# A small copy ahead of ScalarE's loads, and every second rounding moved to GpSimd

## Chip, core and metric

The kernel runs on one core of a Trainium2 chip. The metric is the device time of one execution in microseconds (us); smaller is better. Before the change the median of three runs is 163.75 us (163.68 to 163.84).

## What is computed

A linear layer with a low-rank addition (LoRA with a diagonal), on 16 x 2048 = 32768 rows of 256 float32 numbers:

```python
def reference(x, W, lora_A, lora_B, lora_E, scale):
    x_flat = x.reshape(-1, in_dim)          # 32768 x 256
    y = x_flat @ W                          # W: 256 x 256
    lora_out = x_flat @ lora_A              # 256 x 16
    lora_out = lora_out * lora_E
    lora_out = lora_out @ lora_B            # 16 x 256
    y = y + scale * lora_out
    return y.reshape(batch, seq_len, out_dim)
```

Input and output are 33.5 MB each, so at least 67 MB pass between the chip's memory (HBM) and the core's on-chip memory (SBUF).

## The kernel before

The low-rank part is folded into the weights once: weff = W + A · diag(E · scale) · B (lines 177 to 191 and 238 to 246). Then out = x · weff, so each row of x goes through the core once.

Each of the 128 partitions handles 256 rows of x, which are cut into six blocks (BLOCKS, line 11). They pass through one ring in SBUF, which has room for 184 rows per partition (RING, line 12); a "row" below is one row per partition, 128 KB in all. A result overwrites its input's place in the ring, and the store is issued from there.

All large transfers stand in one list, ORDER (line 13), which SyncE issues from top to bottom: "L16" loads the next 16 rows, "S64" stores the next 64, "W" loads the weights. Three kinds of waits lie in it:

- a store waits until ScalarE has written the last of its rows (semaphore s_c, line 140);
- the load of row 184, the first that reuses places of the ring, waits until the first store has landed (line 137); the load of rows 240 to 255 waits for the second store;
- at the end SyncE waits for all stores of the last four pieces (line 263).

```python
ORDER = [
    "L8", "W", "L8", "L16", "L16", "L16", "L16", "L16", "L24", "L24", "L16", "L24",
    "S64", "S32",
    "L8", "L16", "L16", "L16", "L16",
    "S64", "S24", "S40", "S32",
]
```

Ahead of the list stands a group of early transfers (lines 115 to 120): the first load on SyncE's queue, and lora_A, lora_E and lora_B on ScalarE's queue.

Compute goes by steps of eight rows (G), 32 in all. In each step:

1. VectorE (DVE) rounds eight rows of the ring from float32 to bfloat16, into one of two buffers xb (line 167). It waits for the load where a step begins one.
2. TensorE (PE) transposes them, in eight transposes into PSUM (line 212); pairs of bfloat16 travel as one float32. The last of them counts up s_t.
3. VectorE copies the result from PSUM into one of two buffers xt (line 172).
4. TensorE multiplies by weff, sixteen products per step (line 228).
5. ScalarE copies the products from PSUM into the ring, four rows at a time (line 202), and counts up s_c where a store's rows end.

TensorE's order is fixed by a loop (lines 251 to 256): transposes of step n+1 always come before the products of step n. VectorE's order is: copy of step n, rounding of step n+2 (lines 193 to 195). The buffers are handed over by tokens that TensorE takes and returns (k_x, k_t, k_y). GpSimd (POOL) only makes the identity matrix for the transposes at the start (lines 145 to 155).

The change and the steps of the prediction touch the early group (115), the loop that issues ORDER (129), rounded (158), copied (169) and the loop that calls both (193).

Of the kernel before, what the change touches and what calls it, by code (L numbers as in the profile page):

```python
# [11 lines left out]
RING = 184  # L12
# [6 lines left out]
G = 8  # L19
H = 4  # L20
# [3 lines left out]
def kernel(  # L24
# [10 lines left out]
    nc = tc.nc  # L35
# [4 lines left out]
    x_flat = x.flatten_outer_dims()  # L40
    out_flat = out.flatten_outer_dims()
# [19 lines left out]
    xbs = [const.tile([P, G, K], BF16, name=f"xb_{i}") for i in range(2)]  # L61
# [22 lines left out]
    sem = lambda name: tc.alloc_semaphore(name)  # L84
    s_load = {f: sem(f"load_{f}") for f, _ in loads}

    s_last = sem("stores")
    s_store = {f: sem(f"store_{f}") for f, _ in stores if f < ROWS - RING}
# [4 lines left out]
    s_t, s_m, s_c = sem("s_t"), sem("s_m"), sem("s_c")  # L93
    k_x, k_t, k_y = ([sem(f"{k}_{i}") for i in range(2)] for k in ("k_x", "k_t", "k_y"))
    s_setup = sem("s_setup")

    def rows_of(flat, f, n):
        first, rows = block_of[f]
        block = flat[first * P:(first + rows) * P, :].rearrange("(p b) k -> p b k", b=rows)
        return block[:, f - first:f - first + n, :]  # L100

    def place(f, n):
        return ring[:, f % RING:f % RING + n, :]

    steps = list(range(0, ROWS, G))
    NS = len(steps)
# [2 lines left out]

    def load(f, n):
        return nc.sync.dma_start(out=place(f, n), in_=rows_of(x_flat, f, n)).then_inc(s_load[f], 16)

    early = [
        load(*loads[0]),
        nc.scalar.dma_start(out=a_sb, in_=lora_A.rearrange("(p c) r -> p c r", c=KC)).then_inc(s_in, 16),
        nc.scalar.dma_start(out=e_sb, in_=lora_E[:, None]).then_inc(s_in, 16),
# [7 lines left out]

    with tc.tile_critical():  # L127

        for kind, f, n in queue[1:]:
            if kind == "W":  # L130
                nc.sync.dma_start(
                    out=w_sb, in_=W.rearrange("(p c) m -> p c m", c=KC)
                ).then_inc(s_w, 16)
            elif kind == "L":
                for g, m in stores:
                    if g < f + n - RING and f - RING < g + m and g in s_store:
                        nc.sync.wait_ge(s_store.pop(g), 16)
                load(f, n)
            elif kind == "S":
                nc.sync.wait_ge(s_c, stores.index((f, n)) + 1)  # L140
                nc.sync.dma_start(out=rows_of(out_flat, f, n), in_=place(f, n)).then_inc(
                    s_store.get(f, s_last), 16
                )

        nc.gpsimd.memset(ident_f, 0.0).then_inc(s_setup, 1)  # L145
        nc.gpsimd.wait_ge(s_setup, 1)
        nc.gpsimd.affine_select(  # L147
            out=ident_f,
            in_=ident_f,
            compare_op=mybir.AluOpType.not_equal,  # L150
            fill=1.0,
            base=0,
            pattern=[[-1, P]],
            channel_multiplier=1,
        ).then_inc(s_setup, 1)


        def rounded(n):

            if n == NS:  # L160

                nc.vector.sem_inc(k_x[n % 2], 1)
            if n >= NS:
                return
            if steps[n] in s_load:
                nc.vector.wait_ge(s_load[steps[n]], 16)
            nc.vector.tensor_copy(out=xbs[n % 2], in_=place(steps[n], G)).then_inc(k_x[n % 2], 1)  # L167

        def copied(n):

            nc.vector.wait_ge(s_t, n + 1)
            nc.vector.tensor_copy(  # L172
                out=xts[n % 2].rearrange("p g r c -> p (g r c)"),
                in_=pts[n % 2].rearrange("p g r -> p (g r)").bitcast(BF16),
            ).then_inc(k_t[n % 2], 1)

        nc.vector.wait_ge(s_in, 48)
        nc.vector.tensor_copy(out=b_bf, in_=b_sb)  # L178
        nc.vector.wait_ge(s_setup, 3)
        nc.vector.tensor_scalar(  # L180
            out=ate,
            in0=ps_at,
            scalar1=e_sb,
            scalar2=float(scale),
            op0=mybir.AluOpType.mult,
            op1=mybir.AluOpType.mult,
        ).then_inc(s_setup, 1)
        rounded(0)
        nc.vector.wait_ge(s_w, 16)
        nc.vector.wait_ge(s_setup, 5)  # L190
        nc.vector.tensor_add(out=weff, in0=w_sb, in1=ps_aeb).then_inc(s_setup, 1)  # L191
        rounded(1)
        for n in range(NS):
            copied(n)
            rounded(n + 2)


        for k in k_y:
            nc.scalar.sem_inc(k, 1)
        for h in range(ROWS // H):  # L200
            nc.scalar.wait_ge(s_m, h + 1)
            nc.scalar.copy(out=place(h * H, H), in_=pys[h % 2]).then_inc(k_y[h % 2], 1)  # L202
            if (h + 1) * H in store_ends:
                nc.scalar.drain().then_inc(s_c, 1)  # L204


        def take(token):
            nc.tensor.wait_ge(token, 1).then_inc(token, -1)  # L208


        def transpose(b, j):
            return nc.tensor.transpose(  # L212
                pts[b][:, j, :], xbs[b][:, j, :].bitcast(FP32), ident_f
            )

        def transposes(b):
            take(k_x[b])
            for j in range(G):
                t = transpose(b, j)
            t.then_inc(s_t, 1)  # L220

        def products(b):
            take(k_t[b])
            for j in range(G):
                if j % H == 0:
                    take(k_y[j // H])
                for c in range(KC):
                    m = nc.tensor.matmul(  # L228
                        pys[j // H][:, j % H, :],
                        xts[b][:, j, :, c],  # L230
                        weff[:, c, :],
                        start=(c == 0),
                        stop=(c == KC - 1),
                    )
                if j % H == H - 1:
                    m.then_inc(s_m, 1)

        nc.tensor.wait_ge(s_setup, 2)
        nc.tensor.wait_ge(s_in, 48)
        for c in range(KC):  # L240
            t = nc.tensor.transpose(ps_at[:, c, :], a_sb[:, c, :], ident_f)  # L241
        t.then_inc(s_setup, 1)
        nc.tensor.wait_ge(s_setup, 4)
        for c in range(KC):
            m = nc.tensor.matmul(ps_aeb[:, c, :], ate[:, c, :], b_bf, start=True, stop=True)  # L245
        m.then_inc(s_setup, 1)
        transposes(0)
        nc.tensor.wait_ge(s_setup, 6)
        left = nc.tensor.alloc_register("left")
        nc.tensor.reg_mov(left, NS // 2)  # L250
        with nc.tensor.While(left):
            transposes(1)
            products(0)
            transposes(0)
            products(1)
            nc.tensor.reg_sub(left, left, 1)

        total = nc.sync.alloc_register("total")
        nc.sync.reg_mov(total, n_last)
# [39 lines left out]
```

## Time and profile before

| What | us |
|---|---|
| median of three runs | 163.75 |
| the profiled execution's own time | 163.49 |
| its span, first to last instruction | 161.7 |
| PE busy | 91.0 (56% of the span) |
| DVE busy | 76.4 (47%) |
| ACT busy | 63.1 (39%) |
| POOL busy | 0.7 |
| moved by DMA | 67.42 MB, 417 GB/s over the span |

How to read it: the page is one execution under the hardware profiler; its durations are set against its own 163.49 us, which is 0.26 us below the median of the runs. An engine's share of busy time tells little by itself. What matters is what ends last in each stretch, and whether an engine's wait delays anything behind it. Names such as SPq or ACTq are the sequencers that issue DMAs and waits; q1 is SyncE's DMA queue, q10 ScalarE's.

### The profile page before, as it was taken

The numbers are of one execution on the slowest core, as the hardware profiler recorded it, in microseconds if no ns is written. First come the engines' busy times: TensorE is split into PE (matmuls) and PEld (weight loads), VectorE is DVE, ScalarE is ACT, GpSimd is POOL, SyncE is SP. The second block draws the span as 40 slices with busy tenths as digits, with TensorE's granted clock in tenths as the row PEclk, the third lists the DMA queues.
The fourth block names the chain that finished last, engine by engine and source line by source line (L and its number), as shares of the span: only waits on it lengthen the run. The fifth ranks groups of instructions, "written<-read, shape, count | busy, mean of one in ns | idle before, by whom it ended". The sixth has DMA issues, their size and how long they took to land. (4 is left out here: it accounts for less than half of the span.)

```text
span 161.7 us, 1972 instructions
## 1 busy us (share of the span) xinstructions
PE 91.0 (56%) x780; PEld 81.5 (50%) x780; DVE 76.4 (47%) x67; ACT 63.1 (39%) x65; POOL 0.7 (0%) x6
## 2 busy tenths in 40 slices
PE   0188999999999999970000079999994000000000
PEld 0066899999799999960000066999993000000000
DVE  0296999985889988800000048999930000000000
ACT  3004486868586868680000005768685000000000
POOL 1000000000000000000000000000000000000000
PEclk9999999999999999996555558999999555555555
DMA  5999999999999999799699999999899799899992
GB/s 179 417 426 450 413 434 442 417 458 426 432 415 438 432 521 456 324 519 470 300 413 407 440 421 446 424 421 571 357 486 470 340 395 488 381 466 442 405 421 113
DMA packets 3522, 67.42 MB, mean 417 GB/s; under 512 B 560, under 2 KB 576, under 8 KB 704
## 3 DMA queue, kind: packets, MB, share of 16 engines
q1 hardware_dynamic: 3312, 67.37, 97.6%
q10 hardware_dynamic: 208, 0.03, 0.1%
q14 instruction: 2, 0.02, 0.0%
HBM read 33.85 MB, written 33.55 MB: 417 GB/s over the span
## 5 line engine op out<-in xcount | busy, mean ns | idle before, releaser
L202 ACT COPY ring<-py 128x1024 f32<-128x1024 f32 x64 | 61.8, 1017 | 58.6 <-PE py L228 58.5
L228 PE MATMUL py<-weff,xt 128*128 128x256 bf16 x512 | 62.2, 275 | 0.7 <-PEq L208 0.7
L228 PEld LDWEIGHTS py<-weff,xt 128*128 128x128 bf16 x512 | 50.5, 99 | 7.4 <-issue 1.5
L167 DVE CAST xb<-ring 128x2048 bf16<-128x2048 f32 x32 | 39.0, 1220 | 31.8 <-DMA ring<-in_x_dram 31.5
L212 PE MATMUL pt<-ident_f,xb 128*128 128x128 f32 x264 | 36.7, 286 | 24.0 <-PEq L208 23.9
L212 PEld LDWEIGHTS pt<-ident_f,xb 128*128 128x128 f32 x264 | 31.7, 148 | 25.9 <-issue 25.6
L172 DVE COPY xt<-pt 128x2048 bf16<-128x2048 bf16 x32 | 39.1, 1221 | 4.5 <-PE pt L212 4.4
L241 PE MATMUL py<-ident_f,a_sb 128*16 128x128 f32 x2 | 0.6, 396 | 6.8 <-DMA b_sb<-in_lora_B_dram 6.8
L241 PEld LDWEIGHTS py<-ident_f,a_sb 128*16 128x16 f32 x2 | 0.1, 88 | 6.8 <-issue 6.8
L178 DVE CAST b_bf<-b_sb 16x256 bf16<-16x256 f32 x1 | 0.3, 282 | 6.7 <-DMA b_sb<-in_lora_B_dram 6.7
L202 ACT ACT_TABLE_LOAD x1 | 1.3, 1283 | 2.4 <-issue 2.4
L245 PE MATMUL py<-b_bf,ate 16*128 16x256 bf16 x2 | 0.6, 402 | 0.6 <-DVE ate L180 0.6
L180 DVE TENSOR_SCALAR ate<-py,e_sb 16x256 bf16<-16x256 f32 x1 | 0.5, 472 | 0.5 <-PE py L241 0.5
L191 DVE TENSOR_TENSOR weff<-w_sb,py 128x512 bf16<-128x512 f32 x1 | 0.7, 669 | 0.0
L245 PEld LDWEIGHTS py<-b_bf,ate 16*128 16x128 bf16 x2 | 0.1, 104 | 1.1 <-DVE ate L180 1.1
L147 POOL TENSOR_SCALAR_AFFINE_SELECT ident_f<-ident_f 128x128 f32<-128x128 f32 x1 | 0.3, 294 | 0.2 <-POOL ident_f L145 0.2
L145 POOL MEMSET ident_f<- 128x128 f32 x1 | 0.2, 205 | 1.0 <-SPq L127 1.0
L280 POOL MEMSET const-bfloat16-1.0<- 128x1 bf16 x1 | 0.1, 102 | 0.0
L280 POOL MEMSET const-uint8-127<- 128x1 uint8 x1 | 0.1, 102 | 0.0
L280 POOL MEMSET const-float32-0.0<- 128x1 f32 x1 | 0.1, 99 | 0.2 <-issue 0.2
L280 POOL MEMSET const-float32-1.0<- 128x1 f32 x1 | 0.1, 99 | 0.0
## 6 DMA issues: line engine op xcount, KB each, us to landing
ring<-in_x_dram SPq DMA_DIRECT2D x10, 2048.0 KB, 21.3
ring<-in_x_dram SPq DMA_DIRECT2D x3, 3072.0 KB, 42.5
out_dram<-ring SPq DMA_DIRECT2D x2, 4096.0 KB, 40.0
out_dram<-ring SPq DMA_DIRECT2D x1, 5120.0 KB, 37.4
ring<-in_x_dram SPq DMA_DIRECT2D x3, 1024.0 KB, 7.2
out_dram<-ring SPq DMA_DIRECT2D x1, 3072.0 KB, 39.1
w_sb<-in_W_dram SPq DMA_DIRECT2D x1, 256.0 KB, 5.1
out_dram<-ring SPq DMA_DIRECT2D x2, 43.1
```

The costliest lines, as they stand in the source:

```text
L147: nc.gpsimd.affine_select(out=ident_f, in_=ident_f, compare_op=mybir.AluOpType.not_equal, fill=1.0, base=0, pattern=[[-1, P]], channel_mul ...
L167: nc.vector.tensor_copy(out=xbs[n % 2], in_=place(steps[n], G)).then_inc(k_x[n % 2], 1)
L172: nc.vector.tensor_copy(out=xts[n % 2].rearrange("p g r c -> p (g r c)"), in_=pts[n % 2].rearrange("p g r -> p (g r)").bitcast(BF16),).the ...
L178: nc.vector.tensor_copy(out=b_bf, in_=b_sb)
L180: nc.vector.tensor_scalar(out=ate, in0=ps_at, scalar1=e_sb, scalar2=float(scale), op0=mybir.AluOpType.mult, op1=mybir.AluOpType.mult,).the ...
L191: nc.vector.tensor_add(out=weff, in0=w_sb, in1=ps_aeb).then_inc(s_setup, 1)
L202: nc.scalar.copy(out=place(h * H, H), in_=pys[h % 2]).then_inc(k_y[h % 2], 1)
L212: return nc.tensor.transpose(pts[b][:, j, :], xbs[b][:, j, :].bitcast(FP32), ident_f)
L228: m = nc.tensor.matmul(pys[j // H][:, j % H, :], xts[b][:, j, :, c], weff[:, c, :], start=(c == 0), stop=(c == KC - 1),)
L241: t = nc.tensor.transpose(ps_at[:, c, :], a_sb[:, c, :], ident_f)
L245: m = nc.tensor.matmul(ps_aeb[:, c, :], ate[:, c, :], b_bf, start=True, stop=True)
L280: nc = _bacc.Bacc("TRN2", target_bir_lowering=False, num_devices=1)
```

## The change

It has two parts.

First, a transfer from x in HBM straight into out in HBM, 64 KB in 16 pieces of 4 KB, stands first in ScalarE's queue. It covers the first 64 rows of 256 numbers, all of which the first store writes again; so that store waits for the copy (semaphore s_in0).

Second, GpSimd does the rounding of steps 3, 5, 7 and so on to 31; VectorE keeps the even steps and step 1. GpSimd waits for the transposes of the step that last used the buffer (s_t) and for the load. The token that VectorE gave after the last step stays.

The list freed takes the place of a pop from s_store; SyncE's transfers and their other waits are in the same order as before.

```diff
     early = [
+        nc.scalar.dma_start(out=out_flat[0:16 * H, :].rearrange("(p b) k -> p b k", b=H),
+                            in_=x_flat[0:16 * H, :].rearrange("(p b) k -> p b k", b=H)).then_inc(s_in0, 16),
         load(*loads[0]),
...
+        freed = []
...
-                    if g < f + n - RING and f - RING < g + m and g in s_store:
-                        nc.sync.wait_ge(s_store.pop(g), 16)
+                    if g < f + n - RING and f - RING < g + m and g not in freed:
+                        freed.append(g)
+                        nc.sync.wait_ge(s_store[g], 16)
                 load(f, n)
             elif kind == "S":
+                if f == 0:
+                    nc.sync.wait_ge(s_in0, 16)
                 nc.sync.wait_ge(s_c, stores.index((f, n)) + 1)
...
+        seen = []
+
+        def caster(n):
+            return nc.gpsimd if n % 2 == 1 and n >= 3 else nc.vector
+
+        def rounded(n, engine):
+            piece = max(f for f in s_load if f <= steps[n])
+            waits = [(s_load[piece], 16)]
+            for sem_, count in waits:
+                if (engine, sem_) not in seen:
+                    seen.append((engine, sem_))
+                    engine.wait_ge(sem_, count)
+            engine.tensor_copy(out=xbs[n % 2], in_=place(steps[n], G)).then_inc(k_x[n % 2], 1)
+
+        for n in range(NS):
+            if caster(n) is nc.gpsimd:
+                nc.gpsimd.wait_ge(s_t, n - 1)
+                rounded(n, nc.gpsimd)
...
         for n in range(NS):
             copied(n)
-            rounded(n + 2)
+            if n + 2 < NS and caster(n + 2) is nc.vector:
+                rounded(n + 2, nc.vector)
+            elif n + 2 == NS:
+                nc.vector.sem_inc(k_x[NS % 2], 1)
```

More of the change, by code (lines that the diff above doesn't have):

```diff
@@ L95 @@
     s_setup = sem("s_setup")
+    s_in0 = sem("s_in0")
     def rows_of(flat, f, n):
@@ L155 @@
         ).then_inc(s_setup, 1)
[L158 to L167, printed above, removed]
+        seen = []
[13 more added lines that the diff above has]
+                rounded(n, nc.gpsimd)
         def copied(n):
@@ L187 @@
         ).then_inc(s_setup, 1)
-        rounded(0)
+        rounded(0, nc.vector)
         nc.vector.wait_ge(s_w, 16)
@@ L191 @@
         nc.vector.tensor_add(out=weff, in0=w_sb, in1=ps_aeb).then_inc(s_setup, 1)
-        rounded(1)
+        rounded(1, nc.vector)
         for n in range(NS):
             copied(n)
-            rounded(n + 2)
+            if n + 2 < NS and caster(n + 2) is nc.vector:
+                rounded(n + 2, nc.vector)
+            elif n + 2 == NS:
+                nc.vector.sem_inc(k_x[NS % 2], 1)
         for k in k_y:
```

## The prediction

> **What bounds the kernel now.** I read the slices of the page and its table of DMA queues first, because the kernel moves 67 MB and does little arithmetic on each byte:
>
> ```profile
> DMA  5999999999999999799699999999899799899992
> ...
> q1 hardware_dynamic: 3312, 67.37, 97.6%
> q10 hardware_dynamic: 208, 0.03, 0.1%
> ```
>
> The 16 DMA engines are busy from the first slice to the last, and SyncE's queue (q1) alone fills 97.6% of their span. ScalarE's queue (q10) carries almost nothing. Next the busy time by stretches of the span; the columns are PE, PEld, DVE, ACT, POOL, granted clock, DMA share, GB/s:
>
> ```profile
> 4.00:58.00 54.00, 48.70 (x417) 43.52 (x418) 44.55 (x41) 31.17 (x33) 0.00 (x0) 1.00 1.01 431
> 58.00:90.00 32.00, 13.62 (x125) 12.41 (x123) 9.46 (x9) 11.24 (x12) 0.00 (x0) 0.75 0.99 425
> 112.00:160.00 48.00, 10.99 (x101) 9.97 (x99) 6.07 (x6) 9.31 (x10) 0.00 (x0) 0.64 0.96 415
> ```
>
> The rate is 431 GB/s while PE works nearly all the time and 415 GB/s when PE is idle for three quarters of it: the transfers don't wait for compute. Third, the packet records under this view. Packets of one size take one time (8 KB 309 ns, 2 KB 84 ns, 64 KB 2418 ns) and each engine starts one where the one before ended. The first packet starts at 1.77 us; the engines end between 158.7 and 160.2 us. So **the time is one stream of packets on each engine**, and an edit counts only if it lengthens that stream, moves its start, or leaves it empty.
>
> The page's chain that ended last (PE L228 9%, PE L212 4%) stops at 124.1 us, with ScalarE's last copy; the remaining 36 us are the stores in flight. SyncE's waits say the same; columns are total us, times, longest:
>
> ```profile
> SPq L141 <- ACTq L204: 70.2, 5, 26.9
> SPq L113 <- DMA out_dram<-ring: 39.6, 2, 33.4
> SPq L263 <- DMA out_dram<-ring: 35.8, 1, 35.8
> ```
>
> The 70.2 us look alarming but are waits ahead of a full queue. How full, the timeline of ScalarE (end of a block's last copy, after which its store is issued) against the packet records tells:
>
> ```profile
> 33.41 1.93 ACT L202 COPY ring<-py 128x1024 f32<-128x1024 f32 x2 [0.69 <-PE py L228]
> ...
> 70.78 1.93 ACT L202 COPY ring<-py 128x1024 f32<-128x1024 f32 x2 [0.69 <-PE py L228]
> 97.65 2.08 ACT L202 COPY ring<-py 128x1024 f32<-128x1024 f32 x2 [24.95 <-PE py L228]
> ...
> 122.16 1.93 ACT L202 COPY ring<-py 128x1024 f32<-128x1024 f32 x2 [0.69 <-PE py L228]
> ```
>
> The first store (64 rows) is issued at 35.4 us and its first packet starts at 59.5: 24 us of cover. The second is issued at 46.6 and starts at 78.8: 32 us. The fifth (40 rows) is ready at about 113.6 and starts at 137.0: 23 us. The last is issued at 124.1 and starts at 149.1: **25 us**. Between 72.7 and 97.65 compute stands still because the ring is full (the load of row 184 lands at about 92), which is another 19 us of cover for the first ten of the moved casts.
>
> **The change part by part.**
>
> *GpSimd casts.* 15 of 32 casts (steps 3, 5, ... 31) move from DVE to POOL. DVE loses 15 x 1.220 = 18.3 us of work. That is worth nothing: PE sets the pace of compute, as the chain shows,
>
> ```profile
> 102.04 0.87 PE pt L212 x8
> 102.91 1.75 PE py L228 x16
> ```
>
> so a step is 0.87 + 1.75 = 2.62 us, two are 5.24, and even compute is hidden. What POOL needs for a cast of 128 x 2048 no row of before shows. The nearest rows:
>
> ```profile
> L167 DVE CAST xb<-ring 128x2048 bf16<-128x2048 f32 x32 | 39.0, 1220 | 31.8 <-DMA ring<-in_x_dram 31.5
> ...
> L147 POOL TENSOR_SCALAR_AFFINE_SELECT ident_f<-ident_f 128x128 f32<-128x128 f32 x1 | 0.3, 294 | 0.2 <-POOL ident_f L145 0.2
> L145 POOL MEMSET ident_f<- 128x128 f32 x1 | 0.2, 205 | 1.0 <-SPq L127 1.0
> L280 POOL MEMSET const-bfloat16-1.0<- 128x1 bf16 x1 | 0.1, 102 | 0.0
> ```
>
> One element costs POOL 0.10 us and 128 cost 0.205, so 0.8 ns each after the first: 0.1 + 2048 x 0.0008 = 1.8 us. By the affine select, (294 - 102) / 127 = 1.5 ns each: 3.2 us. With nothing fixed, 16 x 294 ns = 4.7 us. Ends 1.2 (DVE's row) and 4.7; I take 3.2, the one POOL row that reads and writes. The new wait: POOL's cast of step n waits for the transposes of step n-2 (s_t) and its load. Nothing but later casts is queued behind it on POOL. Those who wait for it are PE's transposes of n, and behind them PE's products of n-1. From the end of transposes n-2 to the start of transposes n PE does two sets of products and one of transposes: 1.75 + 0.87 + 1.75 = 4.37 us. 3.2 us fit. At 4.7, with some 0.3 for hand-overs, a pair of steps becomes 0.87 + 5.0 = 5.9 instead of 5.24: 15 x 0.65 = 10 us of compute later, inside the cover. Cost: **0**. Without cover each us by which a pair grows costs 15 us.
>
> The Trainium skill (SBUF — State Buffer, "Who interferes with whom") speaks against moving a cast: GpSimd and a DVE instruction in a 2-port mode exclude each other for a whole instruction. No run shown has both at work, so this trace can't tell. By it one DVE cast (1.22 us) per pair would stand ahead of POOL's, and as an estimate the pair would be 0.87 + 0.3 + 4.7 + 1.22 = 7.1 us, which the cover still absorbs, so the sum stays.
>
> *The copy.* ScalarE issues one DMA more, ahead of three that took 0.41, 0.45 and 0.44 us, so those and what follows move by about 0.45 us: b_sb lands at 7.1 instead of 6.7, DVE's first work and the table load (2.44 us) shift likewise. All of that is compute, under 24 us of cover: 0. SyncE's queue isn't passed by it. The new wait of SyncE (s_in0 ahead of the first store) is met some 30 us early.
>
> The transfer itself has no cover: it runs on the same engines. The DMA view of the first 5 us has 138 packets of q10 among 143 of q1, so the queues share the engines. 16 pieces of 4 KB are one packet on each engine. Between 84 ns (2 KB) and 309 ns (8 KB), 4 KB take 84 + 225/3 = **0.16 us**. But it writes HBM in the midst of loads, and a turn of direction has a price in the packets: where the loads first give way to stores (57.4 to 58.8 us), 14 of the 24 KB packets took 0.09 to 0.31 us more than 0.914, in all 2.5 us, or **0.16 us** per engine. The next such turn (110 us) cost one engine 0.33 and the others nothing. So the turn is 0 to 0.33; I take 0.16, because the copy is the first write to out, as the first turn was. The worst row is the start: first packets of 8 KB took 0.4 to 1.03 us instead of 0.309, some 0.47 over on the mean; if the copy pays this anew, it costs 0.16 + 0.47 = 0.63, at the worst 0.16 + 0.72 = 0.9. If it takes that delay over from the load, and early, it costs less than nothing: 0.16 - 0.47 = -0.3.
>
> *Bookkeeping.* The list freed replaces pop; SyncE's waits and transfers stay in order: 0.
>
> Sum: 163.49 (profiled execution; span 161.7 and 1.8 around it) + 0.16 + 0.16 = 163.81. The median of the runs is 0.26 above the profiled one, so **164.07, rounded 164.1 us**. A measurement of this kernel tells about 0.2% (0.33 us) from no change; the forecast lies on that edge, and I count it as slower.
>
> **The rivals.**
> 1. *The copy is only its bytes, or hides in part*: no turn is paid, 0 to +0.2 us, 163.75 to 163.95. For it: 128-byte packets of q10 among loads take 13 ns, so queues are mixed without a stall. Against it: these write SBUF, not HBM.
> 2. *The copy takes over the cold start (other side)*: 16 descriptors may reach the engines sooner than the load's 128; then the 0.47 us that first packets lose run before the load, and the stream starts smoothly: -0.3 to -0.5, 163.25 to 163.45. It decides if the copy's packets start at least 0.3 us ahead of 1.77. Against it: both queues issue at 0.74 us, and q10's first packet in before came 0.47 us after q1's.
> 3. *The copy is not overlapped at all*: each engine waits for it as for a first packet, 0.63 to 0.9 us: 164.4 to 164.65. The Trainium skill (DMA: Bandwidth & Descriptors, "Latency and other measured facts") gives some 800 ns as the least round trip to HBM; no run here isolates it, and by it the sum would be +0.8.
> 4. *GpSimd becomes the bound*: cover is 19 + 25 = 44 us over 15 casts, 3.0 us a pair; so a pair beyond 8.2 us, a cast beyond 7 us with hand-overs, empties the queue ahead of the last store. A cast of 7.5 us would give 15 x 0.5 = 7.5 us: 171. Against it: all POOL rows scale to under 5.
>
> A smaller unknown: in the 64-row stores, one engine's five successive packets took 2.51 to 2.58 us instead of 2.418 while compute ran, and two such engines end 0.6 us after the rest. More engines at work beside the stores can move the end by some 0.5 us either way.
>
> **How the numbers follow.** Forecast (turn paid, +0.25 to +0.5) 0.34; rival 1 0.32; rival 2 0.17; rival 3 0.10; rival 4 0.07. Slower: the forecast without its lowest fifth (0.28), rivals 3 and 4: 0.45. Within 0.2%: 0.06 + 0.32 = 0.38. Faster 0.17. The range runs from 163.5 (rival 2 is mostly left out) to 165.0 (rival 3 and 0.4 of drift in the late engines are in, rival 4 is out); the two left out hold some 0.2.
>
> **What would show it.** Right: one 4 KB packet per engine of about 0.16 us, a stream without gaps, the engines' end 0.3 us later, POOL casts under 5 us, the last store issued before 149 us. Wrong: the load's first packets shorter than 0.4 us behind the copy (rival 2), copy packets near 1 us (rival 3), a late slice of the DMA row below 9 with SyncE waiting at L149 for ScalarE (rival 4).

## The result and the profile after

The changed kernel takes 163.91 us (median of 20 runs, 163.68 to 164.02), the kernel before beside it 163.62 us (median of 20, 163.51 to 163.88). The ratio is **1.0015, 95% interval 1.0008 to 1.0022**: slower by 0.25 us by the ratio, 0.13 to 0.36 (0.29 by the medians). That is a real loss, but inside the 0.2% that the prediction took as the limit of what can be told. The profiled execution took 163.89 us, its span 162.1. Medians in this text are over all executions; the ratios leave out the one slow execution that occurred, 191.42 us in pool_x4.

The slices and queues of the page after:

```profile
DMA  5999999999999999699699999999899789899992
...
q1 hardware_dynamic: 3312, 67.37, 97.4%
q10 hardware_dynamic: 240, 0.10, 0.2%
```

The stream on SyncE's queue is as full as before. ScalarE's queue grew by 32 packets: 16 pieces of 4 KB, and 16 that count up the semaphore. The same stretches of the span as before (length, PE, PEld, DVE, ACT, POOL, clock, DMA share, GB/s):

```profile
4.00:58.00 54.00, 47.06 (x398) 42.35 (x399) 33.92 (x31) 30.61 (x32) 15.61 (x8) 1.00 1.02 431
58.00:90.00 32.00, 15.71 (x144) 14.35 (x142) 10.25 (x9) 12.64 (x14) 3.79 (x2) 0.78 0.99 424
112.00:160.00 48.00, 11.57 (x106) 10.48 (x104) 5.41 (x5) 9.64 (x10) 1.90 (x1) 0.66 0.96 415
```

DVE gave up a quarter of its work in the first stretch, POOL took it, and the rates of the transfers are within 1 GB/s of before. The groups of casts on the page after:

```profile
L178 POOL CAST xb<-ring 128x2048 bf16<-128x2048 f32 x15 | 29.9, 1992 | 83.9 <-PE pt L235 54.4
...
L178 DVE CAST xb<-ring 128x2048 bf16<-128x2048 f32 x17 | 20.7, 1217 | 24.2 <-DMA ring<-in_x_dram 24.1
```

POOL needs 1.90 us for a cast where nothing holds it up (1.99 on the mean), and sits idle 84 us, 54 of them for PE: it waits for PE, not PE for it. PE's pace in the chain is still 0.87 + 1.75 us a step:

```profile
102.61 0.87 PE pt L235 x8
103.48 1.75 PE py L251 x16
```

SyncE's waits after (total us, times, longest; L149 is the issue of a store, L148 the wait of the first store for ScalarE, which before stood with the others, L286 the wait for the last):

```profile
SPq L149 <- ACTq L227: 43.1, 4, 12.8
SPq L115 <- DMA out_dram<-ring: 37.6, 2, 31.1
SPq L286 <- DMA out_dram<-ring: 35.6, 1, 35.6
SPq L148 <- ACTq L227: 29.7, 1, 29.7
```

The waits for ScalarE come to 43.1 + 29.7 = 72.8 us, against 70.2 before. The first store is issued at 38.2 us instead of 35.4, the last at 124.7 instead of 124.1. Their first packets start at 59.6 and 149.4, so 21 and 25 us of cover are left. The surprise is in ScalarE's first instructions (start, duration):

```profile
0.74 0.63 ACTq L118 DMA_DIRECT2D out_dram<-in_x_dram  x1
1.41 0.59 ACTq L121 DMA_DIRECT2D a_sb<-in_lora_A_dram  x1
2.02 0.58 ACTq L122 DMA_DIRECT2D e_sb<-in_lora_E_dram  x1
2.64 0.47 ACTq L123 DMA_DIRECT2D b_sb<-in_lora_B_dram  x1
```

The copy's first packet starts only at 4.56 us by the packet records, 3.8 us after its issue began; lora_A's first packet in before came 1.5 us after its own. What stands behind the copy waits as well: lora_B is there at 9.6 us instead of 6.7.

The packet records tell a part of where the time went. They don't name the engine; packets that follow each other end to start are taken as those of one engine. 12 of the copy's 16 packets took **159 ns**, the others 176 to 329. As a mean over the 16 engines, the first half of the loads (to row 184) ends 0.14 us later than before (52.35 against 52.21 us), and the last store 0.25 us later (159.46 against 159.21); the latest engine ends at 160.58 against 160.22. The 0.14 us are not simply carried to the end, though: when the first store ends the difference is 0.06 us (79.17 against 79.11), and it is larger only behind the turn from loads to stores at 109 us (111.07 against 110.80).

### The profile page after: what moved, and what is told of

It reads as the page before. It is cut to its first block, busy times and chain, and to the rows that moved or that the text cites. A ratio compares the mean times of both kernels' runs of the same rounds, so it can differ in the third digit from the quotient of the medians.

```text
span 162.1 us, 1988 instructions
## 1 busy us (share of the span) xinstructions
PE 91.8 (57%) x780; PEld 82.8 (51%) x780; DVE 59.8 (37%) x52; ACT 63.2 (39%) x65; POOL 30.6 (19%) x21
## 5 line engine op out<-in xcount | busy, mean ns | idle before, releaser
L251 PE MATMUL py<-weff,xt 128*128 128x256 bf16 x512 | 64.0, 280 | 0.0
L251 PEld LDWEIGHTS py<-weff,xt 128*128 128x128 bf16 x512 | 51.5, 101 | 6.9 <-issue 0.2
L178 POOL CAST xb<-ring 128x2048 bf16<-128x2048 f32 x15 | 29.9, 1992 | 83.9 <-PE pt L235 54.4
L178 DVE CAST xb<-ring 128x2048 bf16<-128x2048 f32 x17 | 20.7, 1217 | 24.2 <-DMA ring<-in_x_dram 24.1
## 6 DMA issues: line engine op xcount, KB each, us to landing
out_dram<-ring SPq DMA_DIRECT2D x1, 3072.0 KB, 38.2
```

The lines of the kernel that those rows point to most:

```text
L178: engine.tensor_copy(out=xbs[n % 2], in_=place(steps[n], G)).then_inc(k_x[n % 2], 1)
L251: m = nc.tensor.matmul(pys[j // H][:, j % H, :], xts[b][:, j, :, c], weff[:, c, :], start=(c == 0), stop=(c == KC - 1),)
```

## The experiments

Theory A: the copy's packet, 0.16 us on each engine in a stream without gaps, is the whole cost. Theory B: GpSimd, or compute that ends later beside the stores, costs something of its own. For it spoke the profile after: at the turn from loads to stores at 109 us, 14 of the 16 KB packets took 0.07 to 0.30 us over their 0.61, where before had none. (Before's one late packet in these loads, 0.33 us over, came at 104 us; the prediction put it at the turn.) Theory C: the late setup costs it. Each ratio is against the kernel before in the same rounds; it is not the quotient of the two medians. Times below are medians. The edits are shown against the changed kernel, those of bare against the kernel before.

### control

The kernel before, with nothing changed.

> The kernel before against itself. Every theory expects a ratio of 1.000; its distance from 1 and its interval show what five rounds can tell, which is wanted beside effects of 0.1 to 0.2%.

163.60 against 163.60 us, ratio 0.9998 (0.9989 to 1.0007). So five rounds tell a change of about 0.1%.

### copy_only

```diff
-            return nc.gpsimd if n % 2 == 1 and n >= 3 else nc.vector
+            return nc.vector
```

> The copy, with all 32 casts on VectorE. Theory A (the cost is the copy's own 4 KB packet on each DMA engine, 159 ns in the profile after, laid into a stream without gaps): all of the cost is here, +0.16 to +0.25 us, ratio 1.0010 to 1.0015. Theory B (GpSimd's casts, or compute that ends later beside the stores, cost it through the turn from loads to stores at 110 us, where 14 packets took 0.07 to 0.38 us more in the profile after): 1.0000 to 1.0005, and that turn is cheap again, one late packet as before.

163.75 against 163.60 us, ratio 1.0007 (0.9998 to 1.0016): +0.11 to +0.15 us, what theory A asks for, though the interval touches 1. In the packets, most of the copy's pieces took 159 to 164 ns, the first half of the loads ends 0.18 us later than in before on the mean, and the turn at 109 us has no late packet, as before. The turn at 58 us, from the first loads to the first stores, was paid again: 21 of the 24 KB packets took 0.09 us or more over their 0.914, 5.1 us in all, where before had 14 and 2.5 us. So the copy hadn't taken it over.

### pool_only

```diff
     early = [
-        nc.scalar.dma_start(out=out_flat[0:16 * H, :]...).then_inc(s_in0, 16),
...
-                if f == 0:
-                    nc.sync.wait_ge(s_in0, 16)
```

> GpSimd's 15 casts, without the copy. Theory A: 0 within the noise, ratio 1.000, setup back at 6.7 us, GpSimd casts of 1.9 us, first store issued at 35.4 us. Theory B: +0.1 to +0.25 us, 1.0008 to 1.0015, with many late packets at the turn of 110 us.

163.67 against 163.60 us, ratio 1.0000 (0.9991 to 1.0009). GpSimd costs nothing that these rounds can tell, up to 0.15 us. But its profile had the late packets at 109 us that theory B speaks of (11 of 16 KB, 0.07 to 0.45 us over), so B was not yet dead. And without any copy the engines of this profile end 0.30 us later on the mean than those of before (159.51 against 159.21), though at row 184 the two are level (52.22 against 52.21). So a difference of 0.1 to 0.3 us between two single profiles does not tell a cause; the ratios over many executions have to.

### copy_64k

```diff
-        nc.scalar.dma_start(out=out_flat[0:16 * H, :].rearrange("(p b) k -> p b k", b=H), ...
+        nc.scalar.dma_start(out=out_flat[0:16 * 64, :].rearrange("(p b) k -> p b k", b=64), ...
```

> As after, but the copy has 16 pieces of 64 KB (its first 1024 rows, all stored again later). Theory A: a 64 KB packet takes 2.42 us on each engine as in the stores, so +2.4 us over before and +2.26 us over after, ratio 1.0148, and whatever else the copy costs does not grow. If a piece from HBM to HBM pays for reading and for writing it would be +4.8 us (1.029). If the copy's price is a turn or a start that it pays once, +0.2 us (1.001 to 1.002).

166.16 against 163.60 us, ratio 1.0161 (1.0133 to 1.0189): +2.6 us, 2.2 to 3.1. The engines' mean end moved by 2.41 us over before. The size of the piece sets the price: its 64 KB packets took 2.45 us, the stores' 2.42. A piece from HBM to HBM is paid once, not for reading and writing apart, and no fixed price larger than the interval shows beside it.

### copy_last

```diff
     early = [
-        nc.scalar.dma_start(out=out_flat[0:16 * H, :]...).then_inc(s_in0, 16),
         load(*loads[0]),
...
         nc.scalar.dma_start(out=b_sb, in_=lora_B).then_inc(s_in, 16),
+        nc.scalar.dma_start(out=out_flat[0:16 * H, :]...).then_inc(s_in0, 16),
```

> As after, but the copy stands behind the three small loads in ScalarE's queue. Theory A (bytes): the same 16 packets of 159 ns in the same stream, ratio 1.0007 to 1.0015, as after; the setup gets its loads early again (b_sb lands near 6.7 us, first store issued near 35.5). Theory C (the copy costs because it holds back lora_A, lora_E and lora_B by 2.9 us): 1.0000.

163.81 against 163.60 us, ratio 1.0013 (1.0004 to 1.0022), while the setup ran on time again; VectorE's first cast (start, duration, and after the bracket what it waited for):

```profile
6.73 0.28 DVE L196 CAST b_bf<-b_sb 16x256 bf16<-16x256 f32 x1 [6.73 <-DMA b_sb<-in_lora_B_dram]
```

So the loss doesn't come from the late setup: theory C falls, up to the 0.1 us that the rounds can't tell. The copy's first packet again came late after its own issue (2.14 to 6.17 us).

### copy_sbuf

```diff
-        nc.scalar.dma_start(out=out_flat[0:16 * H, :].rearrange("(p b) k -> p b k", b=H),
+        nc.scalar.dma_start(out=ring[0:16, RING - H:RING, :],
                             in_=x_flat[0:16 * H, :].rearrange("(p b) k -> p b k", b=H)).then_inc(s_in0, 16),
...
             elif kind == "L":
+                if f + n == RING:
+                    nc.sync.wait_ge(s_in0, 16)
```

> As after, but the 16 pieces of 4 KB go from x into a free place of the ring instead of into out, so nothing is written to HBM early. Theory A: still a 4 KB packet of 159 ns per engine, ratio 1.0007 to 1.0015. If writing HBM amid loads had a price of its own (the turn of the prediction), 0.16 us less than after: 1.0000 to 1.0005 only if the packets are cheaper. It also tells whether the copy's late first packet (4.6 us after the span's start, where lora_A came at 2.2 before) belongs to HBM as a target: then it is back near 2.2 us here.

164.20 against 163.60 us, ratio 1.0037 (1.0023 to 1.0050): +0.6 us, more than twice the loss with HBM as target. I had expected no more than after. Two things are seen in its packets. The first piece is back at 2.30 us, so the late start does belong to the copy into HBM, and the issue takes 0.41 us again instead of 0.63. And the pieces now fall into the cold start: the first took 0.455 us, lora_A's go behind them, and as a mean over the engines the first load ends at 5.34 us (5.07 before), the second at 8.77 (8.30 before). That is 0.47 us lost in the first 9 us. At the end of the third load it is 0.50 (13.68 against 13.18), where after, whose small loads come late, lost 0.10. That the same 4 KB cost more there because the engines' first reads are waiting in front of them is my reading; what the engines wait for at the start wasn't tried apart.

### pool_x3 and pool_x4

```diff
+            for again in range(2 if engine is nc.gpsimd else 0):      # 3 in pool_x4
+                done.append(n)
+                engine.tensor_copy(out=xbs[n % 2], ...).then_inc(s_again, 1)
+                engine.wait_ge(s_again, len(done))
             engine.tensor_copy(out=xbs[n % 2], ...).then_inc(k_x[n % 2], 1)
```

> As after, but GpSimd makes each of its casts three times, each waiting for the one before: 3 x 1.90 and some 0.2 for the waits, 5.9 us. A pair of steps becomes 0.87 + 0.3 + 5.9 = 7.1 us, 1.8 more than 5.24, below the 3.0 that the cover allows: ratio to before as after, 1.001 to 1.002, although compute ends tens of us later in its first part. If the casts are on the path after all, 15 x 1.8 = 27 us.

> As after, but each of GpSimd's casts four times: 4 x 1.90 and some 0.3, 7.9 us, a pair of 9.1 us, 3.8 to 4.0 more than 5.24. The cover ends at 3.0 to 3.3 a pair, so the last store is issued late: 15 x 0.6 to 0.9, +8 to +15 us, 172 to 179 us, and the DMA slices ahead of the last stores fall below 9. If there is more cover than worked out, 164.

Three casts: 164.83 against 163.60 us, ratio 1.0066 (1.0049 to 1.0083). Four: 189.96 us (188.23 to 191.42), 1.1567 (1.1509 to 1.1626). The edge of the cover lies where it was worked out, between the two, but both came out dearer than expected, for two reasons.

First, the casts hold each other up. The timelines of GpSimd and of VectorE in pool_x4:

```profile
37.80 5.81 POOL L182 CAST xb<-ring 128x2048 bf16<-128x2048 f32 x3 [2.15 <-PE pt L241]
43.67 2.76 POOL L184 CAST xb<-ring 128x2048 bf16<-128x2048 f32 x1
```

```profile
40.85 1.23 DVE L196 COPY xt<-pt 128x2048 bf16<-128x2048 bf16 x1 [1.85 <-PE pt L241]
42.00 2.69 DVE L184 CAST xb<-ring 128x2048 bf16<-128x2048 f32 x1
```

VectorE's cast starts while GpSimd is casting and takes 2.69 us instead of 1.22: it ends at 44.7, after GpSimd's third cast (43.6) and one cast of its own. GpSimd's fourth starts at 43.67 and takes 2.76 instead of 1.90: it has to wait for VectorE. VectorE's copy out of PSUM beside GpSimd's casts takes its usual 1.23. The Trainium skill (SBUF — State Buffer, "Who interferes with whom") says just this of a DVE instruction in a 2-port mode and GpSimd, that the second to start waits until the first ends; these rows agree, though no row names the mode in which VectorE's cast ran. From there to the end, GpSimd's first casts of succeeding pairs start 9.9 or 10.8 us apart (37.80 and 48.59, then 58.50), 10.3 on the mean, instead of the 9.1 expected: one cast of VectorE more. The last store is so issued at 175.7 us. In before its first packet started at 149.1, with the queue full; 175.7 - 149.1 = 26.6 us is about the loss measured (26.4 by the medians). The page of pool_x4 shows the empty queue that rival 4 foretold (the slices of DMA; the zeros lie at 77% of the span, two slices of 5 ahead of them at 57%):

```profile
DMA  6999999999999999799999955999793003993595
```

Second, pool_x3 lost 1.1 us over before by the ratio (0.8 to 1.4) with a full queue. Its last store was issued at 136.3 us, 13 us ahead of its first packet, and the mean end of the engines is that of after (159.48 us). But one engine ends at 161.64, 1.83 us behind the next. It is the late engine of the prediction: each of the other profiles with compute has, in each of its two 64-row stores, a row of about five 64 KB packets of 2.47 to 2.58 us instead of 2.418, each starting where the one before ended, so on one engine, as long as compute runs beside the stores and no longer. In pool_x3 the rows go on in the packets behind: between 80 and 89 us, where before has one (0.06 us over), six 32 KB packets took 0.06 to 0.13 us over 1.213, and the second row lasts to 132 us instead of 124.

### after_again and copy_again

> The changed kernel once more, on the same chip and beside the same runs of before as the next three. Theory A (the copy's packet is all): equal to copy_again. Theory B (GpSimd adds something of its own at the turn from loads to stores): 0.1 us above copy_again.

> The copy with all casts on VectorE, once more, to halve the uncertainty of its share: +0.11 to +0.25 us over before, ratio 1.0007 to 1.0015.

The changed kernel: 163.93 against 163.63 us, ratio 1.0017 (1.0008 to 1.0026). The copy alone: 163.80 us, 1.0012 (1.0002 to 1.0021). This time the profile of the changed kernel had no late packet at the turn of 109 us, not 14, and the time was the same within 0.02 us. So those late packets come and go, and theory B in that form falls. The times themselves came out as B had expected, though: the two lie 0.13 us apart, where theory A expected them equal, and 8 of the 11 executions of the changed kernel lie above all 11 of the copy alone. Against that, the intervals of the two ratios overlap, pool_only shows no such share, and copy_last, with the copy and GpSimd's casts both, took 163.81 us. So theory A is borne out for 0.15 to 0.17 us, not for the whole cost: what the other 0.1 us comes from, or whether it is there, stays open.

### bare and bare_copy

```diff
                 elif kind == "S":
-                    nc.sync.wait_ge(s_c, stores.index((f, n)) + 1)
+                    for g, m in loads:
+                        if f <= g < f + n:
+                            nc.sync.wait_ge(s_load[g], 16)
...
-            nc.vector.tensor_copy(out=xbs[n % 2], in_=place(steps[n], G)).then_inc(k_x[n % 2], 1)
...
-            nc.scalar.copy(out=place(h * H, H), in_=pys[h % 2]).then_inc(k_y[h % 2], 1)
...
-            transposes(1)
-            products(0)
```

All instructions of GpSimd, VectorE, TensorE and ScalarE's copies are left out, so out receives x. Each store is then issued as soon as its loads have landed, which is earlier than in before; compute and this issue time change together.

> The kernel before with its compute left out: all transfers in the same order, each store waiting for the loads of its rows instead of for ScalarE, so out receives x. If the DMA stream alone sets the time: no more than 1 us below before (0.994 to 1.000). If the one late engine (64 KB store packets of 2.5 to 2.6 us instead of 2.418, only while compute runs) is due to compute, these slow packets are gone, the engines end within 0.6 us of each other and the time falls by 0.6 to 1.0 us; if it is an engine that is slow by itself, they stay and the time is 1.000.

> As bare, with the 16 pieces of 4 KB from x into out first in ScalarE's queue; compute left out as there. The disputed cost by itself: theory A +0.14 to +0.16 us over bare. If the copy's price came from compute that starts later, it equals bare.

Without compute: 162.63 against 163.63 us, ratio 0.9946 (0.9932 to 0.9960). With the copy: 162.78 us, 0.9956 (0.9942 to 0.9970). The copy by itself costs 0.15 us by the medians and 0.10 by the mean end of the engines, with nothing to delay: theory A's size, though these two intervals overlap. And compute (with the later issue of the stores) costs the stream 0.7 to 1.1 us (0.54% of 163.6, with its interval) though it never leaves the queue empty. The stretch of the second 64-row store, in bare (length, POOL, clock, DMA share, GB/s) and then in before (all engines):

```profile
110.00:130.00 20.00, 0.00 (x0) 1.00 1.01 436
```

```profile
110.00:130.00 20.00, 12.99 (x120) 11.82 (x117) 8.04 (x7) 10.62 (x12) 0.00 (x0) 0.88 1.01 436
```

The rate over all 16 engines is the same, 436 GB/s, so no view by stretches shows it. The packets do: bare has not one 64 KB packet above 2.48 us, before has ten; bare's engines end within 0.57 us of each other, before's within 1.49. In bare the late packets at 109 us are there too (4, of 0.06 to 0.25 us), with GpSimd idle, which is one more reason against theory B.

## Why the prediction was right, point by point

- **What bounds the kernel.** Right. Without any compute the time falls by only 0.5%; with 64 KB pieces it grows by the pieces' own packet time, within its interval.
- **GpSimd's casts cost nothing.** Right within 0.1%: ratio 1.0000 for the casts alone; beside the copy, 0.1 us has no cause shown. The cast was mis-sized, 1.90 us against the 3.2 taken, inside the ends 1.2 and 4.7; by the slope of the memset row, the other one worked out, it would have been 1.8. PE's 4.37 us covered it either way.
- **The copy's bytes, 0.16 us.** Right: 159 ns per packet; +0.15 us in copy_only, +0.17 in copy_again, +0.15 in bare_copy, by medians.
- **The turn, 0.16 us.** This term failed. No turn was paid: 12 of 16 packets took just the time of their bytes, the other four 0.36 us more in all (0.02 per engine), and the turn at 58 us was paid later all the same. The term was read from one profile, and it is no fixed price: over the runs here, late packets at the turn at 58 us came to between 0 (copy_sbuf) and 5.1 us in all (copy_only), 0 to 0.32 per engine. Rival 1 described the copy better than the forecast did. That the sum came out near (+0.25 measured, +0.32 forecast) is luck: the pair of changes lost some 0.1 us more than the copy alone, which lies within the intervals and whose cause I can't name.
- **Slower by over 0.2%.** The forecast stood on the edge and I counted it as slower; the measured 0.15% lies on the near side. With the turn left out, +0.16 us, it would have been counted rightly.
- **The setup moves by 0.45 us.** Wrong in size, 2.9 us; the copy's first packets came late and the small loads queued behind. The cover hid it: copy_last has the setup on time and the same loss.
- **Rival 2 (the copy takes over the cold start).** Its condition was that the copy's packets start ahead of 1.77 us; they started at 4.56. copy_sbuf put them at 2.3, which is still behind 1.77, and it cost more, not less; no run met the rival's condition.
- **Rival 3 (nothing overlapped, +0.63 to 0.9).** Not so here: 159 ns. copy_sbuf's +0.6 us comes near its low end, but 11 of its 16 pieces took 159 ns too. The round trip of some 800 ns that the Trainium skill gives (DMA: Bandwidth & Descriptors, "Latency and other measured facts") isn't paid by a packet that stands in a running stream; no run isolates that round trip.
- **Rival 4 (GpSimd becomes the bound).** Didn't happen at 1.90 us. The limit of about 7 us lies between pool_x3 and pool_x4, but the price past it was twice the one expected for pool_x4. The prediction had priced the two engines' casts excluding each other at one cast of VectorE per pair; the expectation of that run left it out, and the run showed it.
- **The late engine.** Named as a smaller unknown of 0.5 us. It seems worth 0.7 to 1.1 us in the kernel before: without compute, and with stores issued earlier, the slow packets and that much time are gone together.

## What to carry to other kernels

Where every DMA engine goes from packet to packet without a gap, expect an added transfer to cost its packet time per engine; here it did so in two places of ScalarE's queue, beside a full queue of SyncE's. Read that time from packets of the next sizes. Work out how far each store's issue lies ahead of its first packet before moving work to a slower engine; that distance, not the engines' busy shares, says what the slower engine may cost. And look at the engines one by one at the end of the stream, since the last one sets the time and the mean rate hides it. Don't take the price of a turn from one profile, or a cause from 0.1 us between two.

## What the runs showed that was not expected

- A transfer from HBM to HBM on ScalarE's queue took 0.60 to 0.63 us to issue, not 0.41, and its first packet came 3.8 to 4.1 us after the issue began; the same pieces into SBUF came after 1.6. Small loads behind it on that queue were held back by 2.7 to 3.4 us.
- While compute runs, one DMA engine is slow in the 64-row stores: 64 KB packets of mostly 2.48 to 2.58 us instead of 2.418, none above 2.48 without compute. The row lies on one engine at a time; of the others' packets at most one was late. What ties that engine to compute, or to the time at which stores are issued, stays open.
- 4 KB per engine cost 0.6 us at 2.3 us after the start (into SBUF), and 0.15 to 0.25 at 4.6 us or later (into HBM). Time and target changed together, so which of the two makes the price isn't shown.
